# A four-layer hybrid trunk with expert lookups: the opening stage gets another order of weight loads, idle memory as landing places, and another order of its last small steps

## The chip, the cores and the metric

One core of one Trainium2 chip runs the whole program. The metric is the device time of one execution in microseconds (us). The core has TensorE (PE; its weight loads are listed apart as PEld), VectorE (DVE), ScalarE (ACT), GpSimd (POOL) and SyncE (SP). Plain loads are issued by SP; gathers, whose rows are picked by an index in on-chip memory, are issued by POOL.

## The reference

256 tokens with 1024 channels pass through four layers. Each layer adds a token mixer and then an expert lookup to the residual stream:

```python
for i in range(DEPTH):                       # 4: HGRN2, FoX, Mamba-2 SSD, HGRN2
    hn = rmsnorm(h, norm_mix[i])
    mix = hgrn2_mixer(...)                   # or fox_mixer, ssd_mixer
    h = h + mix
    ffn = peer_ffn(rmsnorm(h, norm_ffn[i]), peer_w_q[i], peer_keys[i], peer_u[i], peer_v[i])
    h = h + ffn
return rmsnorm(h, norm_final)

def hgrn2_mixer(h, w_in, g_norm, w_out, lb):
    q, f_logit, i_in, gate = split(h @ w_in)             # 1024 x 4096
    f = lb + (1 - lb) * sigmoid(f_logit)
    o = chunk_gla(q / sqrt(128), 1 - f, i_in, log(f))    # gated linear recurrence, 8 heads of 128
    return (rmsnorm(o, g_norm) * silu(gate)) @ w_out     # norm over each head

def peer_ffn(h, w_q, sub_keys, u_tab, v_tab):            # 8 heads, 16 experts of 16384 for each
    s = q . sub_keys                                     # two halves of 128 keys a head
    ...                                                  # top 16 of each half, top 16 of their sums
    act = gelu(h . u[idx]) * softmax(top_s)
    return sum(act * v[idx])
```

Each token looks up 8 x 16 rows of `u` and as many of `v` in each layer. These rows make up most of what the program reads.

## The kernel before

**Stages.** The tokens are two tiles of 128 (`t` = 0, 1). A stage `s` is one tile in one layer, so there are eight. Stage `s` has a part that makes the queries ready (`ready(s)`: norm, mixer, norm, query projection and key scores) and a part that looks the experts up. In the main loop the lookups of stage `s` run while `side(s)` carries out `ready(s + 1)` in small pieces between them. The first stage has nothing to run beside, so `ready(0)` stands alone at the start: it is the opening, or prologue, in which nothing is gathered yet.

**Lookups.** `u` and `v` lie side by side in `uv`, so one gathered row is 2048 numbers. A stage has 64 pairs of gathers, and each gather brings 128 rows, 1 MB, into one of eight buffers `GB[0..7]`. For each pair `dot` (on DVE) multiplies the `u` halves with the tokens, `spread` turns the results into weights (ACT) and TensorE adds the weighted `v` halves up (L1158). `fetches(i)` puts in line the gathers that have a free buffer and whose indices are known. The indices of a head come from `route(s, hh)`, a chain of some thirty small DVE operations; `route_steps(3, ...)` does three steps of it for each pair.

**Weights.** Every weight matrix is cut into units of 128 x 2048 numbers, 1 MB, listed in `stream` in the order of use. For each tile of a layer of the first kind these are 20 units of the mixer (16 for the input projection, 4 for the output) and 8 units of `wq`. In the list, units 0 to 19 are the first tile's mixer, 20 to 27 its queries, 28 to 47 the second tile's mixer. A unit takes two calls of `half`, and each half makes two products of 128 x 128 by 128 x 512, which the trace shows as two PE instructions each, so a unit is eight instructions. Units go to a ring of three buffers (`raw`). The first two units of each `wq` have places of their own (`kept`) and are loaded once for both tiles. `load_to(u + 1 + NRAW)` after unit `u` asks for the unit three further on.

**Memory.** `mix` is a strip of 12,512 numbers in each partition that each mixer divides anew with `al`. In `hgrn` the first 7 D + P numbers hold keys, logs, gates, values, decayed keys, state and attention; from there on lie factors (`E4`, `EI`, `QM`, `KM`, `QX`, `KX`, `TM`) that are read up to `intra`. `GB` is not used before the first gather.

**Order.** A mixer fills a `Plan`: numbered slots, each with TensorE work (`p.pe(n, ...)`) and with work for the other engines (`p.at(n, ...)`). `run` issues a slot's TensorE work, and behind it what that work has left in `deferred` and the slot's other work. The engines take their instructions in the order of issue. In `hgrn`, `heads_out(q)` makes four heads' outputs, `heads_mean` and `heads_scale` norm them, `gates` and `gated` apply the gate, and `heads_turn` transposes them for the output projection (`q` = 0, 1). `state(q)` makes the state that the second tile starts from, only where `t == 0`.

`normed` adds the mixer's output to the stream, squares, takes the root, scales, transposes, and multiplies by the norm's weights. `act` is an ACT instruction; where the function isn't in the loaded table, an ACT_TABLE_LOAD stands ahead of it.

## Time and profile before

| | us |
|---|---|
| median of 3 runs | 3261.1 (3260.72 to 3261.35) |
| the profiled execution: its own time | 3261.91 |
| the profiled execution: its span | 3260.1 |
| PE, DVE, ACT, POOL busy in the span | 2504.8, 2115.6, 1357.4, 1178.9 |
| moved by DMA | 1326.14 MB, 407 GB/s over the span |

The span runs from the first instruction to the last. Times in the lines of the profile are microseconds from its start. A line of the timeline has start, length, engine, line, operation, destination and sources, count, and in brackets how long the engine had been idle before it and what ended that. "SPq" lines are the issue of DMAs on SP, not the transfers. A line of the windows has for each engine the busy time and the number of instructions, then the granted TensorE clock as a share, the share of the 16 DMA engines' time in use, and GB/s. Matmuls are pipelined, so groups of PE lines overlap a little; the chain of waits lays the same time out without overlap.

### The profile page before, as it was taken

What the parts mean: (1) busy time and instruction counts of PE and PEld (TensorE: products, weight loads), DVE (VectorE), ACT (ScalarE), POOL (GpSimd) and SP (SyncE); (2) the same over time, 40 slices, a digit from 0 to 9 for tenths busy, and PEclk for the clock granted to TensorE, in tenths of its full rate; (3) what the DMA queues carried; (4) which work ended last, traced back from release to release, by engine and by line L of the source; (5) the groups of instructions that cost most, each with busy time, mean ns of one, the idle gap of its engine ahead of it and who ended that gap; (6) DMA issues with size and microseconds to landing.
All of it is one profiled execution on the core that took longest, in us unless ns stands there. A gap on an engine that the chain in (4) does not pass through costs nothing.

```text
span 3260.1 us, 30788 instructions
## 1 busy us (share of the span) xinstructions
PE 2504.8 (77%) x8580; PEld 1113.7 (34%) x8580; DVE 2115.6 (65%) x5579; ACT 1357.4 (42%) x3891; POOL 1178.9 (36%) x1030
## 2 busy tenths in 40 slices
PE   8887786877777786888777897877877777775565
PEld 4433333332333433344333443333323333332222
DVE  1367667576575865778656876576665667667764
ACT  3254333253343633477333674244333444333332
POOL 0133334333343433333334333343333334344443
PEclk9999888887989988999889999889888999888777
DMA  7699999999999999999999999999999999999997
GB/s 260 255 421 421 421 421 420 418 418 416 420 413 421 412 416 420 417 421 412 413 421 411 419 421 410 418 401 421 422 420 418 409 419 420 420 405 419 417 416 330
DMA packets 183048, 1326.14 MB, mean 407 GB/s; under 512 B 20320, under 2 KB 20576, under 8 KB 21728
## 3 DMA queue, kind: packets, MB, share of 16 engines
q0 software_dynamic: 147456, 1073.81, 79.8%
q1 hardware_dynamic: 35424, 250.37, 18.8%
q8 instruction: 71, 1.16, 0.1%
q14 instruction: 97, 0.79, 0.1%
HBM read 1323.05 MB, written 1.05 MB: 406 GB/s over the span
## 4 chain that ended last, share of the span: by engine, by line
DMA 56%; PE 17%; DVE 11%; issue 9%; ACT 4%; POOL 3%; POOLq 0%; DVEq 0%; ACTq 0%
DMA arena<-in_uv,ix 56%; PE acc L1158 9%; DVE arena L202 8%; PE pj L236 5%; POOL arena L1129 3%; PE ps L236 3%; ACT dots L215 2%; ACT L215 1%; ACT dg L215 1%; PE ps L240 1%; ACT arena L215 1%; DVE eq L202 0%; DVE si L202 0%; DVE ti L202 0%; DVE af L202 0%
## 5 line engine op out<-in xcount | busy, mean ns | idle before, releaser
L202 DVE SCALAR_TENSOR_TENSOR arena<-arena 128x1024 f32<-128x1024 f32 (+3 forms) x1282 | 1321.1, 1047 | 930.9 <-DMA arena<-in_uv,ix 882.3
L1129 POOL DMA_INDIRECT arena<-in_uv,ix x1024 | 1176.8, 1149 | 2055.2 <-PE acc L1158 1447.5
L1158 PE MATMUL acc<-arena,dg 128*64 128x512 f32 x4096 | 1319.3, 730 | 721.4 <-ACT dg L215 713.1
L1158 PEld LDWEIGHTS acc<-arena,dg 128*64 128x64 f32 x4096 | 486.2, 156 | 1365.1 <-ACT dg L215 1038.0
L236 PE MATMUL pj<-raw,arena 128*128 128x512 f32 x1776 | 837.9, 615 | 4.5 <-DMA raw<-in_ssm 2.7
L215 ACT ACTIVATE dots<-dots 128x2 f32<-128x2 f32 x512 | 103.5, 202 | 1580.2 <-DVE arena L202 1577.0
L236 PEld LDWEIGHTS pj<-raw,arena 128*128 128x128 f32 x1776 | 327.5, 195 | 518.4 <-issue 498.5
L215 ACT ACT_TABLE_LOAD x328 | 420.8, 1283 | 6.8 <-DVE arena L202 0.8
L215 ACT ACTIVATE dg<-m,dots 128x64 f32<-128x64 f32 x1024 | 292.5, 333 | 0.0
L215 ACT ACTIVATE dots<-dots,gs 128x1 f32<-128x1 f32 x1024 | 245.6, 286 | 16.7
L236 PE MATMUL ps<-arena 128*128 128x128 f32 (+3 forms) x992 | 130.0, 287 | 1.8 <-ACT arena L1003 1.4
L236 PEld LDWEIGHTS ps<-arena 128*128 128x128 f32 (+2 forms) x992 | 103.0, 167 | 68.1 <-issue 41.0
L236 PE MATMUL ps<-cst,arena 128*64 128x128 f32 (+4 forms) x832 | 109.1, 316 | 0.0
L240 PE MATMUL ps<-cst,arena 128*128 128x128 f32 x568 | 93.2, 293 | 19.3 <-DVE arena L202 16.5
L240 PEld LDWEIGHTS ps<-cst,arena 128*128 128x128 f32 x568 | 68.2, 149 | 103.2 <-issue 49.5
L236 PEld LDWEIGHTS ps<-cst,arena 128*64 128x64 f32 (+1 forms) x832 | 85.2, 168 | 32.2 <-issue 19.0
L215 ACT ACTIVATE arena<-arena 128x512 f32<-128x512 f32 (+3 forms) x132 | 67.7, 555 | 46.6 <-DVE arena L202 43.9
L202 DVE DVE_READ_ACCUMULATOR arena<-arena 128x1 f32 x1024 | 84.2, 82 | 0.0
L202 DVE FIND_INDEX8 si<-sv,arena 128x8 uint32<-128x128 f32 x256 | 69.7, 284 | 0.0
L202 DVE MAX8 sv<-arena 128x8 f32<-128x128 f32 x256 | 61.7, 283 | 12.3 <-ACT arena L1012 12.2
L236 PE MATMUL pj<-arena 128*128 128x512 f32 x144 | 68.0, 617 | 0.0
L202 DVE COPY gs<-ig 64x16 f32<-64x16 f32 x256 | 52.6, 205 | 4.7
(103 smaller groups left out, 1126.0 us busy)
## 6 DMA issues: line engine op xcount, KB each, us to landing
raw<-in_hg SPq DMA_DIRECT2D x80, 1024.0 KB
raw<-in_ssm SPq DMA_DIRECT2D x64, 1024.0 KB
raw<-in_wq SPq DMA_DIRECT2D x46, 1024.0 KB
raw<-in_fox SPq DMA_DIRECT2D x32, 1024.0 KB
arena<-in_uv,ix POOLq DMA_INDIRECT x1024
arena<-in_wq SPq DMA_DIRECT2D x9, 1024.0 KB
arena<-in_keys SPq DMA_DIRECT2D x4, 1024.0 KB
arena<-in_x SPq DMA_DIRECT2D x2, 512.0 KB
```

Source lines behind the costliest of these rows:

```text
L202: return getattr(nc.vector, name)(o, *a, **k)
L215: nc.scalar.activation(o, i, f, **k)
L236: nc.tensor.matmul(o, w, m, start=start, stop=stop)
L240: nc.tensor.transpose(o, i, ident)
L1129: nc.gpsimd.indirect_dma_start(GB[n % NGB], None, d["uv"], bass.IndirectOffsetOnAxis(ap=got[s, hh][0][:, g, q:q + 1], axis=0))
L1158: nc.tensor.matmul(accs[s][e][g * 64:g * 64 + 64], dg[:, g], v, start=hh == 0 and q == 0, stop=hh == 7 and q == NQ - 1)
```

## The change

The weights of the opening no longer go strictly through the ring in the order of use. `homes` gives seven units other landing places: 3 and 4 land in `GB[0]` and `GB[1]`, 22 to 24 in `GB[5]` to `GB[7]`, and 28 and 29 (the next stage's first two) in `mix` from `SPACE` = 7 D + P on, where the factors were. `order` is written out by hand: units 22 to 24 and the next stage's 28 and 29 come ahead of their place, the second tile's tokens (`x[1]`) and the keys come late. `loads` issues along `order` until a unit needs a ring buffer and none is left; units with a place of their own take no ring buffer.

Only in the opening (`lone`): both `state(q)` move behind the mixer, into the norm that follows, with their copies behind the norm's transposes. The second half's norm over heads (`q` = 1) moves from slots 15 and 16 to slot 14, its `gates` go ahead of the rest of slot 15, its `gated` moves from slot 16 to 15, and a Tanh on a single spare column stands ahead of it. A Sqrt on the spare column stands at the start and between the two squares of the norm behind the mixer. `warm(n)` issues `n` products of zeros, three at the start and two in the norm behind the mixer, after the states. The first norm is issued whole ahead of `trimask` and `m64` on DVE.

```diff
+SPACE = 7 * D + P
...
+    lone = [True]
...
+    homes = {3: GB[0], 4: GB[1], 22: GB[5], 23: GB[6], 24: GB[7]}
+    homes.update({28 + i: mix[:, SPACE + i * UNIT:SPACE + (i + 1) * UNIT] for i in range(2)})
+    order = [*range(9), 22, 9, 10, 11, 23, 12, 13, 14, 24, 15, 16, "x", 17, "keys", 20, 18, 21, 19, 28, 29, 25, 26, 27]
+    order += range(30, len(stream))
+    order.reverse()
...
-    def load_to(n):
-        while pos[0] < min(n, len(stream)):
-            nm, i = stream[pos[0]]
...
+    def loads():
+
+        while order:
+            u = order[-1]
+            if u == "x":
+                nc.sync.dma_start(h[:, 1], d["x"][1])
+            elif u == "keys":
+                nc.sync.dma_start(keys, d["keys"][0].rearrange("p (g k) -> p g k", g=16))
+            else:
+                nm, i = stream[u]
+                keep = nm[0] == "w" and i < NKEPT + (KIND[int(nm[2])] == "fox")
+                if keep:
+                    r = mix[:, LEFT:] if i == NKEPT else at_["kept"][:, i * UNIT:(i + 1) * UNIT]
+                elif u in homes:
+                    r = homes[u]
+                elif pos[0] < NRAW:
+                    pos[0] += 1
+                    r = rawp.tile([P, UNIT], F32, name="raw")
+                else:
+                    return
+                if not keep or (nm, i) not in kept:
+                    nc.sync.dma_start(r, d[nm][i])
...
+                raws[u] = r, keep or u in homes
+            order.pop()
...
         if k:
-            del raws[u]
-            load_to(u + 1 + NRAW)
+            pos[0] -= not raws.pop(u)[1]
+            loads()
...
+        def pre(self, n, f, *a):
+
+            self.ahead.setdefault(n, []).append(lambda: f(*a))
...
+                deferred[:0] = self.ahead.get(n, ())
                 yield from slot(lambda: deferred.extend(fs))
...
                 both = [adds[0], both[0], adds[1], both[1]]
+                if lone[0]:
+                    both.insert(2, lambda: act(spare, eps, AF.Sqrt))
...
-            if t == 0:
+            if lone[0]:
+                carry.setdefault("late", []).append(lambda q=q: state(q))
+            elif t == 0:
                 p.pe(10 + 2 * q, state, q)
             p.pe(11 + 3 * q, heads_out, q)
-            p.at(12 + 3 * q, heads_mean, q)
-            p.at(13 + 3 * q, heads_scale, q)
-            p.at(13 + 2 * q, gates, q)
-            p.at(14 + 2 * q, gated, q)
+            if not (lone[0] and q):
+                p.at(12 + 3 * q, heads_mean, q)
+                p.at(13 + 3 * q, heads_scale, q)
+                p.at(13 + 2 * q, gates, q)
+                p.at(14 + 2 * q, gated, q)
+            else:
+
+                p.at(14, heads_mean, q)
+                p.at(14, heads_scale, q)
+                p.at(14, lambda: act(spare, eps, AF.Tanh))
+                p.pre(15, gates, q)
+                p.at(15, gated, q)
             p.pe(15 + 2 * q, heads_turn, q)
...
-        if t == 0:
+        if s and t == 0:
             nc.sync.dma_start(keys, d["keys"][l].rearrange("p (g k) -> p g k", g=16))
         yield from mixers[KIND[l]](l, t, carry)
-        yield from normed(t, carry["acc"], DEPTH + l, xn)
+        norm = normed(t, carry["acc"], DEPTH + l, xn)
+        if lone[0]:
+
+            for _ in range(2):
+                yield next(norm)
+            for f in carry["late"]:
+                f()
+            copies = deferred[:]
+            deferred.clear()
+            warm(2)
+            for _ in range(5):
+                yield next(norm)
+            deferred.extend(copies)
+        yield from norm
         yield from queries(s)
...
+    def warm(n):
+
+        b = accp.tile([P, 512], F32, name="acc")
+        for _ in range(n):
+            nc.tensor.matmul(b, zeros[:, 0:P], zeros, start=True, stop=True)
...
     nc.vector.memset(eps, EPS)
+    zeros = GB[4][:, 0:512]
+    nc.vector.memset(zeros, 0.0)
+    warm(3)
+    act(spare, eps, AF.Sqrt)
     first = ready(0, None)
     for _ in range(2):
         next(first)
-    load_to(NRAW)
-    nc.sync.dma_start(h[:, 1], d["x"][1])
+    loads()
+    for _ in range(6):
+        next(first)
     nc.vector.tensor_copy(trimask, tri[:, None, :].to_broadcast([P, 4, P]))
     tm(m64, ident[:, 0:64], ident[:, 64:P], op=OP.add)
     while (0, 0) not in scored:
         next(first)
+    lone[0] = False
```

More of the change, by code (lines that the diff above doesn't have):

```diff
@@ L263, in trunk @@
     pos = [0, 0]
-    def load_to(n):
-        while pos[0] < min(n, len(stream)):
-            nm, i = stream[pos[0]]
-            keep = nm[0] == "w" and i < NKEPT + (KIND[int(nm[2])] == "fox")
-            r = (mix[:, LEFT:] if i == NKEPT else at_["kept"][:, i * UNIT:(i + 1) * UNIT]) if keep else \
-                rawp.tile([P, UNIT], F32, name="raw")
-            if not keep or (nm, i) not in kept:
-                nc.sync.dma_start(r, d[nm][i])
-            if keep:
-                kept.add((nm, i))
-            raws[pos[0]] = r
-            pos[0] += 1
+    def loads():
[19 more added lines that the diff above has]
+                    nc.sync.dma_start(r, d[nm][i])
+                if keep:
+                    kept.add((nm, i))
+                raws[u] = r, keep or u in homes
+            order.pop()
     def half(nm, use):
@@ L281, in half @@
         assert stream[u][0] == nm, (stream[u], nm)
-        load_to(u + 1)
-        use(raws[u].rearrange("p (k c n) -> p k c n", k=2, c=2)[:, k])
+        use(raws[u][0].rearrange("p (k c n) -> p k c n", k=2, c=2)[:, k])
         pos[1] += 1
         if k:
-            del raws[u]
-            load_to(u + 1 + NRAW)
+            pos[0] -= not raws.pop(u)[1]
+            loads()
     def project(nm, ub, names):
@@ L336, in __init__ @@
         def __init__(self):
-            self.slots = {}
+            self.slots, self.ahead = {}, {}
         def pe(self, n, f, *a):
@@ L431, in hgrn @@
         top[0] = mark
+        assert top[0] == SPACE
         E4 = al(4 * 512).rearrange("p (h n) -> p h n", h=4)
```

## The prediction

> **What bounds the kernel now.** I read the page first: the span, the rate of the transfers in 40 slices of 81.5 us, and the engines' shares of the chain that ended last.

> ```profile
> span 3260.1 us, 30788 instructions
> ...
> GB/s 260 255 421 421 421 421 420 418 418 416 420 413 421 412 416 420 417 421 412 413 421 411 419 421 410 418 401 421 422 420 418 409 419 420 420 405 419 417 416 330
> ...
> DMA 56%; PE 17%; DVE 11%; issue 9%; ACT 4%; POOL 3%; POOLq 0%; DVEq 0%; ACTq 0%
> ```

> From the third slice to the last but one the transfers run close to 420 GB/s. Only the first two slices and the end fall short. Then I asked for windows at the place where the rate changes:

> ```profile
> 0.00:130.00 130.00, 113.54 (x414) 58.94 (x415) 28.40 (x77) 36.44 (x61) 1.16 (x5) 0.96 0.62 228
> 130.00:140.00 10.00, 10.00 (x28) 4.65 (x27) 4.02 (x16) 3.51 (x8) 4.16 (x5) 1.00 0.73 265
> 140.00:3240.00 3100.00, 2373.10 (x8121) 1047.26 (x8121) 2076.28 (x5474) 1312.09 (x3806) 1173.58 (x1021) 0.89 1.01 417
> ```

> The last column is GB/s, the one before it the DMA share. From 140 us to 3240 us the share is 1.01, the rate 417 GB/s. In the opening it is 0.62 and 228, with TensorE busy 113.54 of 130 us. So the opening is TensorE's and the rest belongs to the transfers. The bytes of the program are fixed (the change adds no transfer). The time is therefore the moment when the transfers become full, plus the bytes still to come at 0.421 MB a microsecond (the full slices), plus a tail that the change does not touch. Two things can shorten it: an earlier first gather, and bytes that were moved before it.

> **The opening step by step.** These are the steps of TensorE ahead of the first gather.

> ```profile
> 4.28 0.63 ACT L215 ACTIVATE arena<-arena 128x512 f32<-128x512 f32 x1 [2.25 <-DMA arena<-in_x]
> ```

> ```profile
> 9.89 11.97 PE L236 MATMUL pj<-raw,arena 128*128 128x512 f32 x24
> 22.15 10.94 PE L236 MATMUL pj<-raw,arena 128*128 128x512 f32 x24 [0.29 <-DMA raw<-in_hg]
> ```

> ```profile
> 67.12 0.44 PE ps L240 x4
> 67.55 3.44 PE pj L236 x8
> 70.99 0.89 PE ps L236 x8
> ```

> The first rows are from the timeline, the last three from the chain of waits. There four transposes take 0.44 us and a unit (eight instructions) takes 3.44 us, 0.43 us an instruction, when nothing holds it. Its transfer takes 1.0486 / 0.421 = 2.5 us.

> *Front.* 24 instructions should take 10.32 us. The first 24 took 11.97 (slow start, 1.65 lost), the next 24 waited 0.29 and took 0.62 too long, because unit 3 stood behind `x[1]` and the keys on SP's queue. Both now come late, and units 3 and 4 need no free ring buffer, so 0.91 goes. What comes ahead of the first product:

> ```profile
> arena<-in_x SPq DMA_DIRECT2D x2, 512.0 KB
> arena<-in_keys SPq DMA_DIRECT2D x1, 1024.0 KB
> cst<-in_const SPq DMA_DIRECT2D x1, 712.0 KB
> par<-in_par SPq DMA_DIRECT2D x1, 448.0 KB
> ```

> The first norm loses a table load, but unit 0 cannot be there before constants, parameters and the unit itself (448, 712 and 1024 KB, 2.24 MB, 5.3 us) have followed the tokens that landed at 4.28, so at 9.6: the product starts 0.3 earlier, not more. The three zero products (six instructions, about 5 us at half clock) lie in time in which TensorE idles, and warm it; they cost nothing as long as they end before the transposes at about 7. The transposes then end at about 7.9 and TensorE idles some 1.7 us until unit 0. Does the clock hold through that? The nearest row is a gap of 2.09 us further down, in the timeline of PE alone, and with it the granted clock (the column behind POOL's) of two windows:

> ```profile
> 87.63 3.70 PE L236 MATMUL pj<-raw,arena 128*128 128x512 f32 x8 [0.67 <-ACT arena L573]
> 93.42 0.63 PE L240 MATMUL ps<-cst,arena 128*128 128x128 f32 x4 [2.09 <-DVE arena L202]
> 93.89 12.16 PE L236 MATMUL pj<-raw,arena 128*128 128x512 f32 x24
> 109.97 1.97 PE L240 MATMUL ps<-cst,arena 128*128 128x128 f32 x8 [3.92 <-DVE arena L202]
> 111.87 8.75 PE L236 MATMUL pj<-arena 128*128 128x512 f32 x16
> ...
> 127.36 10.57 PE L236 MATMUL pj<-raw,arena 128*128 128x512 f32 x24
> ```

> ```profile
> 90.00:100.00 10.00, 7.91 (x19) 3.38 (x18) 2.27 (x4) 1.68 (x3) 0.00 (x0) 0.83 0.84 329
> 110.00:120.00 10.00, 10.00 (x23) 5.14 (x24) 1.69 (x3) 0.00 (x0) 0.00 (x0) 0.74 0.01 5
> ```

> The gap of 2.09 us ends at 93.42, and over the ten microseconds around it the clock was 0.83; behind the 3.92 us it was 0.74. The coming gap is a little shorter, so I take half of the 1.65. Front: 0.3 + 0.8 + 0.9 = 2.0, with ends 1.2 and 2.85.

> [...]

> *States.* `state(q)` is eight small instructions, 0.89 us in the row above, and both lie on TensorE's busy stretch: 1.8 us go. They come back in the norm's pause, below.

> *Second half's heads, and the output projection.*

> ```profile
> 87.60 1.28 ACT L215 ACT_TABLE_LOAD   x1
> 88.89 0.30 ACT L215 ACTIVATE ms<-ms,eps 128x4 f32<-128x4 f32 x1
> 89.21 1.28 ACT L215 ACT_TABLE_LOAD   x1
> ...
> 107.61 1.28 ACT L215 ACT_TABLE_LOAD   x1
> ```

> ```profile
> L202 DVE TENSOR_TENSOR arena<-ps,par 128x512 f32<-128x512 f32 x4 | 2.8, 692 | 1.9 <-PE ps L240 1.9
> ```

> These are ACT in the timeline (PE's rows stand above) and a group of DVE operations on 128 x 512, 692 ns each.

> The root and its table loads move under the last unit of the input projection, where ACT idles. The Tanh then stands ahead of the copy that TensorE waits for, so the projection starts 0.5 us later (88.15 in the old clock of this row); but `gated`, three operations of 0.69 us behind the Tanh, is ready at about 89.6, inside the first 3.44 us. TensorE then runs without a gap: 88.15 + 3.44 + 0.44 (four transposes) + 24 x 0.43 ends at 102.4 instead of 106.05. That is 3.65: the idle 2.09, the half clock behind it (12.16 against 10.32), less the 0.5.

> *Norm's pause.* Before, 106.05 to the first query product at 111.87 are 5.8 us. Without the table load the transposes could start after 3.92 - 1.28 = 2.64 us, but TensorE now has the states (1.8) and two zero products (four instructions, 1.72) first: 3.5. With the transposes at full clock (0.44 for four) and one multiplication of 0.69 the first product comes after 4.85 us: 1.0 gained. If Square needed a table of its own behind the new Sqrt, 1.28 would come back.

> *First queries.* 16 instructions took 8.75 us at a clock of 0.74; with TensorE never idle for long they take 6.88: 1.9 gained. What follows up to the first gather (copies, scores, DVE's routing) stays as it is.

> ```profile
> 134.62 1.08 POOL L1129 DMA_INDIRECT arena<-in_uv,ix  x1 [132.92 <-DVE ix L202]
> ...
> 161.34 0.94 POOL L1129 DMA_INDIRECT arena<-in_uv,ix  x1 [16.09 <-PE acc L1158]
> ```

> Sum: 2.0 + 1.8 + 3.65 + 1.0 + 1.9 = 10.3. The first gather (POOL's first row above) goes from 134.6 to 124.3; the second row is the ninth, the first that waits for a buffer.

> **Bytes ahead.** By 130 us the old program had moved 228 GB/s x 130 us = 29.6 MB: 25 units and the small inputs. Then it had stopped, its ring full. The new one has five more units on the chip by then: 25, 26, 27 in the ring, 28 and 29 in scratch, because 22 to 24 lie in `GB`: 5.24 MB. The loads fit. Unit 14 was read at 82.0 (87.63 less 1.3 for transposes and copy, 3.44 for unit 15, 0.9 for the heads' products), and now at 78, front and states earlier. Behind it SP's queue holds 17, the keys, 20, 18, 21, 19, 28, 29, 25, 26, 27: eleven MB or 27 us, all there by 107, and unit 19 within a microsecond of its use. Units 28 and 29 wait for the last reader of the factors, `intra`, which stands ahead of unit 14 in the plan, so SP finds that wait over; 25 to 27 are queued behind. On POOL's queue gathers 5, 6, 7 now wait until units 22, 23, 24 are read. Unit 24 was read by 137.9 (127.36 + 10.57), 3.3 us behind the first gather; gather 7 stands seven issues or at least 7.6 us behind it. So that costs nothing; if unit 24 came more than 4 us late, each further microsecond would be one of POOL's.

> Put together, by 140 us: before, 29.6 + 2.65 = 32.3 MB. After, 29.6 + 5.24 and 14.3 us of full transfers (from 124.3 + 1.4 for issue, an estimate from the 1.08 us of the row) or 6.0 MB: 40.8. Ahead by 8.6 MB, at 0.421 that is 20.4 us.

> **What eats into it.** The ninth gather waits for the first pair, which stands on ACT and PE behind the last key scores, so it moves with the rest: 161.34 - 10.3 = 151.0, its transfer 152.4. The transfers have work from 125.7 for eight gathers and three units (30 to 32), 27.5 us, until 153.2. Just enough. Behind it the pairs run at DVE's pace:

> ```profile
> 174.06 1.22 DVE L202 SCALAR_TENSOR_TENSOR arena<-arena 128x1024 f32<-128x1024 f32 x1
> ...
> 184.21 1.21 DVE L202 SCALAR_TENSOR_TENSOR arena<-arena 128x1024 f32<-128x1024 f32 x1
> ```

> These are the first dots of the fifth and the seventh pair, 10.15 us apart, and two pairs of gathers take 10.0 us of transfers, so nothing is left over for catching up. Six units filled the queue here before, three do now. I take 1.5 us of idle transfers; the ends are 0 and 6 (the units that are missing, less what the earlier data make up). Later stages: the two `kept` units no longer count toward the three asked for ahead, which changes the order in a full queue, not its length: 0, within 1 us.

> 18.9 us in all. The profiled execution had a span of 3260.1 and a time of 3261.9, 0.8 above the median 3261.1. So its span would be 3241.2, and the median **3242**.

> **Rivals.**
> *The first pairs cannot keep up.* The transfers run dry between 150 and 185 us, for the whole 6 us instead of 1.5: 3247. For it: the 0.8 us of reserve above. Against it: in the old trace the dots there waited for data, which now come sooner. 0.17.
> *The clock falls anyway.* The fillers don't hold it: 0.8 of the front, 1.84 of the projection, 1.9 of the queries and 1.1 for cold transposes are lost, 5.6 together: 3248. For it: 2.09 us sufficed before. 0.12.
> *The units ahead don't land ahead*, or their time comes back as waits at the stage ends, so that only the earlier gather counts: 20.4 less 12.5, with the 10.3 whole: 3253. Against it: a DMA share of 1.01 over 3100 us. 0.07.
> *Slower: units 28 and 29 plug SP's queue.* Their wait for scratch ends late, 25 to 27 stand behind, the last queries starve, and with them the first pair and all buffers of the gathers. It costs a microsecond for each that the wait ends beyond about 125 us (unit 25 is wanted at 137.9 - 10.3) and decides from about 145; at 160 us the time is 3242 + 35 = 3277. Against it: the last reader stands ahead of unit 14, some 50 us before that. 0.04.

> **How the numbers follow.** The forecast has 0.58; 0.02 is for what I have not seen. The range 3236 to 3252 takes in the forecast with its upper bounds (2.85 in front, no idle transfers: 3239.9, and some for estimates), the first two rivals, and half of the third. About 0.2% or 6.5 us is what a measurement can tell from no change. Forecast, the first two rivals and most of the third are faster by more: 0.92. Same: 0.04, slower: 0.04.

> **What would show it.** First gather at 124 to 126; 34 to 35 MB by then; no transfers of weights between 108 and the first gather; a granted clock of 1.00 from 90 to 120; PE gaps of 2.09 and 3.92 us gone; DMA share at 1.0 from 130 on, with a dip near 150 to 180 if the first rival holds. A first gather later than 130, or a share under 0.95 between 150 and 190, would prove me wrong in the step concerned.

## The result, and the profile after

The changed kernel takes **3249.82 us** (median of 6 executions, 3249.03 to 3252.91). Before, it was 3261.22 (6 executions, 3260.65 to 3265.65). The ratio is 0.9964, with an interval of [0.9951, 0.9976]: 11.4 us or 0.35% faster, where 19 were forecast. The profiled execution took 3249.74 us, its span 3247.9.

The page of the changed kernel, in the lines that were read of before:

```profile
span 3247.9 us, 30818 instructions
...
GB/s 288 303 420 421 422 421 418 421 416 410 420 409 421 414 416 420 416 421 410 411 422 409 420 418 408 416 417 421 419 414 417 408 421 414 416 412 413 416 418 336
...
DMA 56%; PE 17%; DVE 10%; issue 9%; ACT 4%; POOL 3%; POOLq 0%; SPq 0%; DVEq 0%; ACTq 0%
```

The first two slices are the ones that moved most (260 and 255 GB/s before); no other differs by more than 16. What bounds the rest has not changed. The windows of the same kernel, where the last column is GB/s and the one before it the DMA share:

```profile
0.00:130.00 130.00, 122.30 (x440) 62.15 (x441) 32.71 (x93) 38.27 (x70) 2.41 (x7) 0.99 0.68 268
130.00:140.00 10.00, 10.00 (x36) 5.29 (x35) 3.49 (x12) 1.80 (x4) 7.95 (x7) 1.00 0.97 359
140.00:160.00 20.00, 14.43 (x50) 8.39 (x50) 9.01 (x26) 9.63 (x26) 3.53 (x3) 0.74 1.02 426
160.00:180.00 20.00, 16.90 (x53) 7.06 (x49) 18.35 (x53) 11.05 (x30) 8.76 (x9) 0.91 1.01 417
180.00:200.00 20.00, 20.00 (x60) 6.93 (x60) 11.70 (x33) 14.20 (x30) 8.12 (x8) 1.00 1.01 418
140.00:3230.00 3090.00, 2348.25 (x8100) 1034.95 (x8098) 2073.76 (x5464) 1311.02 (x3804) 1158.20 (x1017) 0.89 1.01 416
```

The first row gives 268 GB/s x 130 us = 34.84 MB, where 34.8 was forecast, against 29.6 before. So the five units are on the chip. Between 140 and 200 us the share is 1.01 and more: the transfers do not run dry behind the first gathers. Most of what is missing is time ahead of the first gather, as the timelines of POOL and of DVE show (start first, length second; the last row is from the chain of waits of the kernel before):

```profile
128.44 1.08 POOL L1168 DMA_INDIRECT arena<-in_uv,ix  x1 [126.75 <-PE pj L237]
```

```profile
127.36 0.17 DVE L203 CAST ix<-gs 128x16 int32<-128x16 f32 x1
```

```profile
134.16 0.17 DVE ix L202
```

The first gather went from 134.62 to 128.44, 6.2 us instead of 10.3. The place of each lost microsecond stands in the timeline of PE:

```profile
1.49 5.42 PE L1240 MATMUL acc<-arena 128*128 128x512 f32 x6 [1.49 <-DVE arena L1248]
7.52 1.09 PE L241 MATMUL ps<-cst,arena 128*128 128x128 f32 x8 [0.61 <-DVE arena L203]
10.32 12.13 PE L237 MATMUL pj<-raw,arena 128*128 128x512 f32 x24 [1.71 <-DMA raw<-in_hg]
22.29 7.03 PE L237 MATMUL pj<-arena 128*128 128x512 f32 x16
...
85.79 3.70 PE L237 MATMUL pj<-raw,arena 128*128 128x512 f32 x8 [0.96 <-ACT arena L602]
89.33 0.60 PE L241 MATMUL ps<-cst,arena 128*128 128x128 f32 x4
89.76 7.30 PE L237 MATMUL pj<-raw,arena 128*128 128x512 f32 x16
98.27 3.70 PE L237 MATMUL pj<-raw,arena 128*128 128x512 f32 x8 [1.21 <-DMA raw<-in_hg]
101.81 1.95 PE L237 MATMUL ps<-arena 128*128 128x128 f32 x16
103.59 1.88 PE L1240 MATMUL acc<-arena 128*128 128x512 f32 x4
105.31 1.04 PE L241 MATMUL ps<-cst,arena 128*128 128x128 f32 x8
106.69 7.13 PE L237 MATMUL pj<-arena 128*128 128x512 f32 x16 [0.34 <-DVE arena L203]
```

The third row is the front: the first 24 instructions still take 12.13 us, and they begin at 10.32, later than the 9.89 of before. The row at 98.27 is a wait that was not there before: TensorE stands 1.21 us for unit 19. The gaps of 2.09 and 3.92 us are gone, the granted clock is 1.00 from 90 to 120 us, and the queries take 7.13 us instead of 8.75. A fourth loss is on POOL: the index is ready at 127.36 + 0.17 = 127.53 and the gather starts 0.91 us later. Before, it was 0.29 (134.33 to 134.62).

### The profile page after: what moved, and what is told of

It is laid out like the page before. It is cut to its first block, busy times and chain, and to the rows that moved or that the text cites. A ratio compares the mean times of both kernels' runs of the same rounds, so it can differ in the third digit from the quotient of the medians.

```text
span 3247.9 us, 30818 instructions
## 1 busy us (share of the span) xinstructions
PE 2486.3 (77%) x8590; PEld 1104.8 (34%) x8590; DVE 2116.8 (65%) x5580; ACT 1356.4 (42%) x3893; POOL 1168.6 (36%) x1030
## 3 DMA queue, kind: packets, MB, share of 16 engines
q1 hardware_dynamic: 35424, 250.37, 18.7%
q8 instruction: 71, 1.16, 0.1%
## 4 chain that ended last, share of the span: by engine, by line
DMA 56%; PE 17%; DVE 10%; issue 9%; ACT 4%; POOL 3%; POOLq 0%; SPq 0%; DVEq 0%; ACTq 0%
DMA arena<-in_uv,ix 56%; PE acc L1197 8%; DVE arena L203 8%; PE pj L237 6%; POOL arena L1168 3%; PE ps L237 3%; ACT dots L216 2%; ACT L216 1%; ACT dg L216 1%; PE ps L241 1%; ACT arena L216 1%; DMA raw<-in_hg 1%; DVE eq L203 0%; DVE si L203 0%; DVE sv L203 0%
## 5 line engine op out<-in xcount | busy, mean ns | idle before, releaser
L1197 PE MATMUL acc<-arena,dg 128*64 128x512 f32 x4096 | 1305.9, 724 | 735.4 <-ACT dg L216 734.4
L237 PE MATMUL pj<-raw,arena 128*128 128x512 f32 x1720 | 808.9, 613 | 7.8 <-DMA raw<-in_ssm 3.9
L237 PEld LDWEIGHTS pj<-raw,arena 128*128 128x128 f32 x1720 | 315.5, 194 | 505.7 <-issue 487.3
L241 PE MATMUL ps<-cst,arena 128*128 128x128 f32 x568 | 89.6, 285 | 5.6 <-ACT arena L1039 3.3
L237 PE MATMUL pj<-arena 128*128 128x512 f32 x200 | 91.3, 603 | 0.3 <-DVE arena L203 0.3
L203 DVE MAX8 sv<-arena 128x8 f32<-128x128 f32 x256 | 61.7, 282 | 12.5 <-ACT arena L1051 12.5
L216 ACT ACTIVATE arena<-ps 128x512 f32<-128x512 f32 (+3 forms) x114 | 43.3, 426 | 29.0 <-PE ps L237 28.4
## 6 DMA issues: line engine op xcount, KB each, us to landing
raw<-in_hg SPq DMA_DIRECT2D x76, 1024.0 KB, 9.1
raw<-in_ssm SPq DMA_DIRECT2D x64, 1024.0 KB, 9.3
raw<-in_wq SPq DMA_DIRECT2D x43, 1024.0 KB, 9.5
raw<-in_fox SPq DMA_DIRECT2D x32, 1024.0 KB, 9.1
arena<-in_wq SPq DMA_DIRECT2D x12, 1024.0 KB, 13.6
arena<-in_hg SPq DMA_DIRECT2D x4, 1024.0 KB, 13.1
arena<-in_keys SPq DMA_DIRECT2D x4, 1024.0 KB, 9.1
```

The lines of the kernel that those rows point to most:

```text
L203: return getattr(nc.vector, name)(o, *a, **k)
L216: nc.scalar.activation(o, i, f, **k)
L237: nc.tensor.matmul(o, w, m, start=start, stop=stop)
L241: nc.tensor.transpose(o, i, ident)
L1197: nc.tensor.matmul(accs[s][e][g * 64:g * 64 + 64], dg[:, g], v, start=hh == 0 and q == 0, stop=hh == 7 and q == NQ - 1)
```

## The experiments

All kernels are edits of the changed kernel. "Lead" is what a kernel has moved by 200 us beyond the 57.62 MB of before, at the 0.421 MB a microsecond of the full slices. These are the DMA lines of the first 200 us: before, the changed kernel, and the best kernel of this study.

```profile
DMA packets 8298, 57.62 MB, mean 288 GB/s; under 512 B 910, under 2 KB 1038, under 8 KB 1550
```

```profile
DMA packets 9131, 63.68 MB, mean 318 GB/s; under 512 B 1004, under 2 KB 1132, under 8 KB 1644
```

```profile
DMA packets 9709, 67.88 MB, mean 339 GB/s; under 512 B 1070, under 2 KB 1198, under 8 KB 1710
```

| kernel | first gather | advance | MB by 200 us | lead | lead less advance | 3260.1 less its span | median | ratio to before |
|---|---|---|---|---|---|---|---|---|
| before | 134.62 | | 57.62 | | | | | |
| changed | 128.44 | 6.2 | 63.68 | 14.4 | 8.2 | 12.2 | 3249.82 | 0.9964 [0.9951, 0.9976] |
| e1_loads | 132.09 | 2.5 | 62.45 | 11.5 | 9.0 | 9.9 | 3251.78 | 0.9968 [0.9956, 0.9980] |
| e2_steps | 125.72 | 8.9 | 61.29 | 8.7 | -0.2 | 8.3 | 3254.38 | 0.9976 [0.9966, 0.9986] |
| e3_no28 | 126.66 | 8.0 | 62.65 | 11.9 | 4.0 | 9.8 | 3251.55 | 0.9966 [0.9954, 0.9978] |
| e4_gap | 128.32 | 6.3 | 63.66 | 14.3 | 8.0 | 14.5 | 3248.12 | 0.9956 [0.9942, 0.9970] |
| a2_again | 126.41 | 8.2 | 64.83 | 17.1 | 8.9 | 18.0 | 3246.68 | 0.9955 [0.9942, 0.9969] |
| e5_order | 124.94 | 9.7 | 65.49 | 18.7 | 9.0 | 18.6 | 3244.49 | 0.9950 [0.9937, 0.9964] |
| e5_both | 124.92 | 9.7 | 65.43 | 18.6 | 8.9 | 19.2 | 3244.38 | 0.9948 [0.9934, 0.9961] |
| e7_all | 138.02 | -3.4 | 61.70 | 9.7 | 13.1 | 12.0 | 3253.38 | 0.9977 [0.9967, 0.9987] |
| e8_nofill | 127.47 | 7.2 | 64.41 | 16.1 | 9.0 | 14.7 | 3247.61 | 0.9955 [0.9942, 0.9969] |
| e9_best | 124.21 | 10.4 | 67.88 | 24.4 | 14.0 | 20.6 | 3240.10 | 0.9932 [0.9919, 0.9946] |

Each ratio goes by runs of before on the same chip at the same time; their medians were 3263.22 for e1 to e4, 3260.88 for a2, e5 and e7, and 3262.55 for e8 and e9. The gather, the lead and the span are those of one profiled execution each. The column "lead less advance" is the one to read: it is what the units ahead are worth once the earlier gather is taken off. It is 8 to 9 us for five units, about 4 for three, 13 to 14 for seven, and nothing for none. The results of e7_all are wrong, as its section says; its row serves for the bytes alone.

**e1_loads: the loads alone.** `homes` and `order` stay, the steps go back to their old places and the fillers go.

```diff
-    lone = [True]
+    lone = [False]
...
-    zeros = GB[4][:, 0:512]
-    nc.vector.memset(zeros, 0.0)
-    warm(3)
-    act(spare, eps, AF.Sqrt)
...
-    for _ in range(6):
-        next(first)
```

> The new landing places and the new order of loads alone; the small steps, states, table loads and zero products are as before. Measured by the MB moved in the first 200 us (before 57.62, changed 63.68, 0.42 MB is one microsecond) and by the time. Theory A (lead at 200 us = bytes landed ahead + earlier first gather, and nothing is given back): first gather at about 134 (134.6 less 0.9 for the waits of the first units, plus 0.6 on POOL), 61.4 MB, 9.0 us faster than before. Theory B (bytes landed ahead come back as waits later, only the earlier gather counts): 61.4 MB, but the time within 2 us of before.

**e2_steps: the steps alone.** No homes, and the loads in the old order.

```diff
-    homes = {3: GB[0], 4: GB[1], 22: GB[5], 23: GB[6], 24: GB[7]}
-    homes.update(...)
-    order = [*range(9), 22, 9, 10, ...]
-    order += range(30, len(stream))
+    homes = {}
+    order = [*range(3), "x", "keys"]
+    order += range(3, len(stream))
```

> The small steps alone (states in the pause, heads, roots and tables, zero products), every unit through the ring in the order of use, the second tile's tokens and the keys behind unit 2 as before. Theory A: first gather at about 127.5 (no wait for unit 19, no extra waits on POOL), 60.5 MB by 200 us, 6.5 to 7 us faster than before; with the loads alone this adds up to the lead of the changed kernel within 1 us. Theory B: the same 6.5 to 7 us, and that is more than half of what the changed kernel gains.

Each alone is faster than before, by 0.32% and 0.24%. For e1_loads that decides between its theories: it gained 11.4 us (interval 6.5 to 14.4) with a gather only 2.5 us earlier, so the bytes ahead counted to the end and did not come back as waits. The leads of the two add to 20.2 us, and the whole change has 14.4. The column shows that the units' part does add up (9.0 and -0.2 against 8.2 to 9.0). It is the advance that doesn't: 2.5 + 8.9 = 11.4 against 6.2. Of the surplus, 1.7 us is counted twice. In e1 the clock happened to hold behind the gap of 2.08 us, so its 24 projection instructions took 10.47 us instead of 12.16, which e2 brings by closing the gap:

```profile
92.53 0.63 PE L241 MATMUL ps<-cst,arena 128*128 128x128 f32 x4 [2.08 <-DVE arena L203]
93.00 10.47 PE L237 MATMUL pj<-raw,arena 128*128 128x512 f32 x24
```

The larger of the other losses come only with both together, or by chance: in e2 the first 24 instructions took 10.54 us, and unit 19 was there. The late start on POOL is no such loss, for e1 has it too (0.91 us).

**e3_no28: units 28 and 29 without a home,** so that they go through the ring.

```diff
-    homes.update({28 + i: mix[...] for i in range(2)})
-    order = [..., 18, 21, 19, 28, 29, 25, 26, 27]
-    order += range(30, len(stream))
+    order = [..., 18, 21, 19, 25, 26, 27]
+    order += range(28, len(stream))
```

> The changed kernel with units 28 and 29 through the ring, so two units (2.1 MB) fewer are there at the first gather. Theory A: first gather within 0.5 us of 128.4, 61.6 MB by 200 us, 5.0 us slower than the changed kernel. Theory B (these bytes come back later): 61.6 MB, but less than 2 us slower.

Its front was the quick one (10.54 us), so its gather came earlier than the changed kernel's. Less the advance, the two units are worth 8.2 - 4.0 = 4.2, or 5.0 against the 9.0 of the other runs, where two transfers of 2.5 us are 5.0. So they land ahead. That they count to the end this run does not show: its gain over before is 11.7 us, against 11.4 and 14.2 (a2_again) with the two units, and the interval of each reaches about 4 us to either side. The 5 us slower that were forecast did not come; the quick front hides at least a part of them.

**e4_gap: the front kept warm.** Two products of zeros behind the transposes of the first norm, in the 1.7 us in which TensorE waits for unit 0.

```diff
     for _ in range(6):
         next(first)
+    warm(2)
```

> The changed kernel with two more zero products behind the first norm's transposes, in the 1.7 us in which TensorE waits for unit 0. If idleness inside a window of 3.4 us, and not a gap as long as that, withdraws the clock, then the first 24 product instructions take 10.3 instead of 12.1 us, the first gather comes at 126.7, 64.4 MB by 200 us, 1.7 us faster than the changed kernel. If the gap is not the cause, they take 12 us still and nothing changes by more than 0.3 us.

Its timeline of PE:

```profile
8.19 1.88 PE L1240 MATMUL acc<-arena 128*128 128x512 f32 x4
10.08 10.54 PE L237 MATMUL pj<-raw,arena 128*128 128x512 f32 x24
...
93.28 3.67 PE L237 MATMUL pj<-raw,arena 128*128 128x512 f32 x8 [1.75 <-DMA raw<-in_hg]
98.15 3.70 PE L237 MATMUL pj<-raw,arena 128*128 128x512 f32 x8 [1.20 <-DMA raw<-in_hg]
```

The front is the quick one, 10.54 us instead of 12.13, and nothing comes of it. (That the filler made it quick this run alone does not show, for e2 and e3 were quick without it; the last section has the busy shares of the front with it and without.) TensorE is 1.8 us ahead up to the projection, and there it waits 1.75 us for unit 18 and 1.20 for unit 19; the first gather is at 128.32, where it was. The projection's last units had become the limit. They stand behind the tokens, the keys, 20 and 21 on SP's queue. Either those loads are in the way, or the ring gives its buffers back too late.

How much that cost here was partly chance, as the next run shows: with the same order and as quick a front TensorE waited there 1.12 us for unit 19 and not for 18. A load lands in 16 shares, each of which the trace records. In e4_gap unit 18 was issued at 82.60, its eighth share landed at 90.28 and its last at 93.14; in a2_again the times are 82.75, 90.46 and 91.23, with the same bytes moved up to then to within 0.1 MB. One share trailed; why, the traces do not show.

**a2_again: the changed kernel once more,** on the chip of the next three.

> The changed kernel once more, so that the three that run with it have it on the same chip. If the clock of the front is set by where the window of 3.4 us falls (the first 24 product instructions took 12.1 us in the changed kernel, 10.5 in a kernel with the same front), this run may have either, and the first gather lies at 128.4 or at 126.6 to 127; the MB by 200 us at 63.7 or 64.4.

The same program, and its first gather came 2.0 us earlier, at 126.41; its timeline of PE says why.

```profile
1.49 4.79 PE L1240 MATMUL acc<-arena 128*128 128x512 f32 x6 [1.49 <-DVE arena L1248]
7.42 1.09 PE L241 MATMUL ps<-cst,arena 128*128 128x128 f32 x8 [1.13 <-DVE arena L203]
10.24 10.54 PE L237 MATMUL pj<-raw,arena 128*128 128x512 f32 x24 [1.73 <-DMA raw<-in_hg]
```

The gap ahead of unit 0 is the same 1.7 us, and here the clock held: it was 1.00 from 10.1 to 13.5 us, where it was 0.50 in the changed kernel. So the front has two outcomes with the same code.

**e5_order: the same loads, the four others earlier.** The tokens, unit 20, the keys and unit 21 are issued from unit 9 on, where the queue has time, instead of among units 17 to 19.

```diff
-    order = [*range(9), 22, 9, 10, 11, 23, 12, 13, 14, 24, 15, 16, "x", 17, "keys", 20, 18, 21, 19, 28, 29, 25, 26, 27]
+    order = [*range(9), 22, 9, "x", 10, 20, 11, 23, 12, "keys", 13, 21, 14, 24, 15, 16, 17, 18, 19, 28, 29, 25, 26, 27]
```

> The changed kernel with the second tile's tokens, the keys and units 20 and 21 asked for earlier (behind 9, 12, 10 and 13), where the transfers idle, so that nothing stands ahead of units 17 to 19. Theory A (the wait for unit 19 comes from what was put ahead of it on SP's queue): no wait for a weight between 85 and 105 us, first gather 1.2 us earlier than in the changed kernel with the same front (127.2, or 125.5 with a warm front), 0.5 MB more by 200 us, 1.2 us faster. Rival (the wait is the ring's: unit 19 can only be asked for when 16 has been read): the wait of 1.2 us stays and so does the first gather.

**e5_both: this order, and the filler of e4.**

> Both the filler of the front and the earlier tokens, keys and units 20 and 21. The filler alone put the first products 1.9 us ahead by 82 us and gave all of it back in waits for units 18 and 19 (1.75 and 1.20). Theory A: with nothing ahead of them on the queue those waits go, first gather at 125.4, 64.9 MB by 200 us, 3 us faster than the changed kernel. Rival (the ring's three buffers set the pace there): the waits stay, first gather at 128.3 and 63.7 MB.

The timeline of PE in e5_order:

```profile
84.03 3.70 PE L237 MATMUL pj<-raw,arena 128*128 128x512 f32 x8 [0.96 <-ACT arena L602]
...
88.00 10.47 PE L237 MATMUL pj<-raw,arena 128*128 128x512 f32 x24
```

The 24 instructions run in 10.47 us without a wait. The first gather comes 1.5 us ahead of a2_again's, with the same number of ring buffers, so the loads ahead on SP's queue were the cause and the ring was not: unit 19 is asked for at 87.76 us, as in a2_again (87.85), and has landed at 92.64 instead of 96.20. In the medians the two runs are not told apart (3244.49 and 3246.68, with ranges that overlap). e5_both is no faster: the front of e5_order was a quick one by itself. The front was quick in all four kernels with the filler, and in four of six with the same front without it, so the count alone proves little; the busy shares in the last section are the better evidence.

**e7_all: two more homes.** `GB[2]` and `GB[3]` for units 3 and 4, so that the first gather's buffer has no earlier user, and two pieces of the strip, 2 D each, for units 30 and 31: logs and gates, values and decayed keys. Order and filler as in e5_both.

```diff
-    homes = {3: GB[0], 4: GB[1], 22: GB[5], 23: GB[6], 24: GB[7]}
+    homes = {3: GB[2], 4: GB[3], 22: GB[5], 23: GB[6], 24: GB[7]}
+    homes.update({30 + i: mix[:, (1 + 2 * i) * D:(3 + 2 * i) * D] for i in range(2)})
```

> A version meant to beat both: the filler, the earlier loads, units 3 and 4 in GB[2] and GB[3] (so that the first gather waits for no reader of them), and units 30 and 31 in the scratch of logs, gates, values and decayed keys, which is free behind the states. Theory A: first gather at 124.8, 37 MB moved by then, 67.4 MB by 200 us, a lead of 23 us over the kernel before, so 3238 to 3240. Theory B (with so many bytes ahead the first pairs cannot keep up and the transfers run dry between 145 and 190 us): a DMA share under 0.95 there, and a lead of 19 us or less.

I had overlooked that `state(q)` reads data in that part of the strip and is issued late. The loads of 30 and 31 were put ahead of it in the program, so the states were made from weights instead of decayed keys and values, which makes the results wrong, and TensorE waited for those weights. One line of its timeline:

```profile
110.50 3.45 PE L237 MATMUL ps<-arena 128*128 128x128 f32 x16 [12.01 <-DMA arena<-in_hg]
```

The wait of 12.01 us is nearly the whole loss (138.02 - 12.01 = 126.0), and the states behind it took 3.45 us instead of 1.95. Even so the lead less advance is 13.1: the seven units were there.

**e8_nofill: without the filler in the norm's pause.**

```diff
-            warm(2)
```

> The changed kernel without the two zero products in the norm's pause; the states stay there. The states end 1.7 us earlier, the transposes are ready at about 2.6 us behind the last product of the projection, so TensorE idles about 0.9 us. If idleness of half a window withdraws the clock (2.09 and 3.92 us did in the kernel before), 0.9 us does not: the granted clock stays at 1.00 from 95 to 120 us, the 16 query instructions take 6.9 us still, and the first gather comes 0.6 us earlier than with the filler. Rival: the clock falls, the 16 instructions take 8 us or more and the first gather comes 1 us or more later.

```profile
104.30 1.06 PE L241 MATMUL ps<-cst,arena 128*128 128x128 f32 x8 [1.15 <-DVE arena L203]
105.71 7.13 PE L237 MATMUL pj<-arena 128*128 128x512 f32 x16 [0.35 <-DVE arena L203]
```

Where the zero products stood, the timeline of PE now has 1.15 us of idling, and the queries still take 7.13 us. So the clock held without this filler (1.00 from 95 to 120 us), and it was not needed. The front was the slow one here (12.02 us), as in the changed kernel, and the first gather came 1.0 us earlier. Of that, 0.6 was there at the projection's end already (101.21 against 101.81); the filler left out is worth the other 0.4, where 0.6 was forecast.

**e9_best: e7 with the two loads held back** until the states have been issued.

```diff
+    held = [True]
...
+            if u == 30 and held[0]:
+                return
...
             for f in carry["late"]:
                 f()
+            held[0] = False
+            loads()
```

> The version meant to beat both, with its mistake mended: in the kernel with 12 us of waiting, units 30 and 31 were asked for ahead of the states, which then waited for them and read them in place of decayed keys and values. Here they are asked for behind the states. Filler, earlier loads, units 3 and 4 in GB[2] and GB[3] as there. Theory A (every MB on the chip at the first gather is worth 2.4 us and nothing comes back): first gather at 124.3, 37 MB moved by then, 67.4 MB by 200 us, a lead of 23 us over the kernel before there and at the end, so 3237 to 3239. Theory B (the first pairs cannot keep up once the transfers have fewer weights between them): DMA share under 0.95 somewhere between 140 and 190 us, lead 20 us or less.

3240.10 us (3239.98 to 3241.93), 22.45 below the 3262.55 of before beside it: the lowest median here. That is twice the 11.4 us measured first for the changed kernel, with intervals that do not meet, and 1.6 times the 14.2 us of its repetition; from e5_both the intervals do not separate it. Its windows behind the first gather:

```profile
140.00:160.00 20.00, 12.36 (x48) 6.86 (x47) 11.49 (x35) 13.77 (x35) 6.75 (x6) 0.82 1.02 423
160.00:180.00 20.00, 19.82 (x60) 8.23 (x56) 18.24 (x51) 9.76 (x28) 9.04 (x8) 0.93 1.01 421
180.00:200.00 20.00, 20.00 (x61) 6.93 (x60) 15.37 (x44) 14.28 (x32) 8.09 (x7) 1.00 1.01 420
```

The share stays above 1 even with the gathers 4.2 us earlier and seven units ahead, so the first pairs keep up here too.

## Why the prediction was right, and where its sum was too large

Direction and mechanism were right: the transfers bound all but the opening, and each megabyte moved earlier came off the end, give or take some microseconds. The range (3236 to 3252) held the time, near the end to which it had been drawn for rivals that did not occur; that much was luck. The forecast was 7.8 us too good, and these are the steps that made it so. In the span it was 6.7: 6.0 too much lead, 2.2 lost behind 200 us, less the 1.5 of idle transfers that did not come. The other 1.1 lie between the profiled executions and the medians.

**Front: 2.0 forecast, about 0.3 in the profiled run.** Half of the clock's loss was to go, and none of it did: 12.13 us against 11.97. This term was a coin, not a half: 12.0 to 12.1 us or 10.5, as the repeated run shows. The other part was a wrong landing time. Unit 0 was to be there at 9.6, and its last share landed at 10.18 (9.66 before), so that the first product started at 10.32. Its first share landed at 9.06 to 9.23 in all twelve traces, the last at 9.65 to 9.79 in three and at 9.91 to 10.18 in the others; the last share of the tokens, the first load of all, trails in the same ones. e2_steps trails with the old loads, and e8_nofill with this front does not, so the new order isn't the reason; why a share trails stays open. Only the waits for unit 3 went nearly as forecast, 0.8 of 0.9.

**States 1.8, projection 3.65.** The states went. The projection ended 4.24 us earlier than before (101.8 against 106.05), of which 2.1 are its own instead of 3.65: 1.2 is the wait for unit 19, and 0.4 lies in the two units ahead of it, 16 instructions in 7.30 us where 6.88 were reckoned. This is the step that failed: "unit 19 within a microsecond of its use", which the sum then put at nothing. I had worked out when the whole queue would be through, and not when each unit would be there; with four loads put ahead of it on SP's queue, unit 19 was not. TensorE was free for it at 97.06, its first share landed at 96.99 and its last at 98.23. In e2_steps, without them, the projection gave 3.9.

**Norm's pause 1.0, queries 1.9.** The pause is 106.69 - 101.81 = 4.88 us, forecast 4.85. The queries gave 1.6. No table had to be loaded anew behind the Sqrt.

**Not in the sum at all: POOL.** 0.91 instead of 0.3 us between index and gather. It goes with `GB[0]` having had an earlier load and readers: it is 0.91 in all eight kernels in which unit 3 lands there and 0.29 in the four in which it doesn't. In e9_best, where the first gather's buffer is fresh, the index is ready at 123.92 and the gather starts at 124.21:

```profile
124.21 1.08 POOL L1172 DMA_INDIRECT arena<-in_uv,ix  x1 [122.52 <-DVE ix L203]
```

Its bracket names the index as what ended the wait; in the changed kernel it names PE.

**Bytes ahead: 34.8 MB by 130 right, 20.4 us of lead too much by 6.0.** 4.1 of it is the later gather. 1.6 more is the start of the transfers, forecast 1.4 us behind the gather's issue. The 3.59 MB of the window 130 to 140 are 8.5 us at the full rate, as if full from 131.5, or 3.0 behind the issue. Before, a unit covered that gap, as this window of the kernel before shows, which ends with the first gather's issue:

```profile
131.00:134.60 3.60, 3.60 (x10) 1.61 (x9) 3.05 (x12) 1.88 (x5) 0.00 (x0) 1.00 0.63 223
```

That is 0.8 MB of unit 25, and POOL issues nothing yet. The units ahead cannot be counted for more than the old kernel's own loads leave. The prediction had this in its 2.65 MB, but not the idle start in its place. By the table, three to seven units are worth 2.5 us each, less 3.5; with none (e2_steps) nothing is lost, for there the old loads run on.

**Starvation 1.5, forecast too high.** It was 0, and the first rival (0.17) is refuted: no dip in the windows from 140 to 200.

**The other rivals.** The clock fell in the front, as the second said (0.50 from 10.1 to 13.5 us), and nowhere else in the opening (1.00 from there to 146.6 us): its time (3248) was nearest to the measured one, but by other terms, of which only 0.8 us came true. The third, that the units don't land ahead or come back as waits, is refuted: by the column of the table for the landing, by e1_loads for the end. Between 200 us and the end the leads lose from -2.3 to 3.8 us, 0.7 in the mean, at no fixed place; in the changed kernel it was 2.2. Executions of one program differ by as much (those of before beside a2_again run from 3258.80 to 3265.29). For e9_best, with 3.8, most of the loss lies between 1500 and 2200 us, and what causes it stays open. The fourth, slower, did not occur: units 28 and 29 held up nothing.

**The median.** The profiled execution of the changed kernel had the slow front. Its repetition ran from 3243.91 to 3248.52 us. The two medians of the one program lie 3.1 us apart, of which the coin in the front can explain 1.6; a forecast of this kernel could hardly be nearer than that.

## What to carry to other kernels

Where transfers bound all but the opening, count bytes moved by a fixed moment: the lead in megabytes, divided by the full rate, is the time at the end (here to within 4 us), and what an earlier start brings and what units ahead bring can be read apart. For every load moved ahead in a queue, work out the landing of each load behind it against its own use, not the moment when the queue is empty: loads that "fit" gave back 1.2 us here, and in e4, where a share trailed too, all that a quicker front had won. And look for memory that is already free: two more units in scratch were worth 5 us of lead, provided that everything that still reads it, the steps one has moved oneself included, stands ahead of the load.

## What the runs showed of the hardware

```profile
6.70:10.10 3.40, 1.30 (x9) 0.86 (x8) 2.80 (x7) 1.33 (x2) 0.00 (x0) 1.00 1.02 427
10.10:13.50 3.40, 3.18 (x4) 1.52 (x5) 0.00 (x0) 0.00 (x0) 0.00 (x0) 0.50 1.00 424
```

PE is busy 1.30 of 3.40 us, 0.38, and the next window runs at half clock. In a2_again PE was no busier in the same stretch of the span, 1.09 us, and the clock held:

```profile
6.70:10.10 3.40, 1.09 (x8) 0.86 (x8) 2.79 (x7) 1.28 (x1) 0.00 (x0) 1.00 1.00 422
10.10:13.50 3.40, 3.26 (x8) 1.61 (x9) 0.00 (x0) 0.00 (x0) 0.00 (x0) 1.00 1.03 434
```

There the grid lay elsewhere, and its windows over the same gap were 0.56 and 0.60 busy. In e8_nofill a window of 0.47 cost the clock. That is the coin. With two products of zeros in the gap of the front, TensorE idled for at most 0.71 us from the first product of zeros to unit 0 in each of the four kernels, so that no window between them was below 0.79, and the clock held in all four: the first 24 instructions took 10.54 us in each.

**The first gather started later where its buffer had a past.** Into a `GB[0]` that had an earlier load and readers it started 0.91 us behind its index, into a fresh one 0.29. It holds for the first gather alone: in e9_best the third and fourth, into `GB[2]` and `GB[3]` where units 3 and 4 had been, start as close behind the one before as all others (0.30 us of idle time). What makes the difference stays open.
